# Four row tiles at once while the weights stream in, and a new order of the first Strassen group

## The chip, the cores and the metric

One core of one Trainium2 chip. The metric is the device time of one execution in microseconds; lower is better. "Faster" and "slower" as verdicts need 2%, which is 30 us here; everything below is about differences of 1 to 10 us, and is settled by the profile more than by the clock on the wall.

## The reference

```python
# x: [8, 2048, 2048] float32, w: [2048, 2048] float32
cs = np.cumsum(x, axis=1)
diff = cs - np.concatenate([zeros, cs[:, :-1, :]], axis=1)   # this is x again
return np.matmul(diff, w)
```

So it is one matmul of 16384 x 2048 by 2048 x 2048. Its rows are cut into 128 tiles of 128 rows, numbered 0 to 127.

## The kernel before

The kernel has two parts. While w comes in (16.8 MB), the first row tiles are multiplied plainly, in bf16, piece by piece of w. Then w is scaled to fp16 in four blocks B11, B12, B21, B22, differences T1 to T4 of them are made, and from tile 4 on groups of four row tiles (g, g+1, and h = g+2, h+1) go through a Strassen-Winograd scheme. The first group of four (tiles 4 to 7) is `group_plain`; the other 30 are `group`, which the change does not touch.

`after(engine, ask)` fixes the order in which an engine is given its instructions; the engine then takes them strictly in that order. The parts that matter, before:

```python
EARLY = 3; PLAIN = EARLY + 1
...
for h in range(2):                       # the two halves of w's columns
    ps = [[bank(2 * r + n) for n in range(2)] for r in range(EARLY)]   # six of eight banks
    for ko in range(KO - KQ):
        ...
            if ko == KQ:                 # three quarters of x are turned here, in one go
                for q in range(1, 4):
                    turn_x(q, cast_x(q))
            taken(h, ko)                 # ScalarE casts a piece of w, VectorE takes its maximum
        ...
        for r in range(EARLY):
            plain(h, r, ko)
    ...
# then: tile 3 is turned alone, and multiplied by the scaled blocks (64 matmuls)
V, X = ([bank(i + n) for n in range(2)] for i in (6, 0))
for a in range(2):
    for h in range(2):
        for k in range(KH):
            for n in range(NH // NB):
                nc.tensor.matmul((V, X)[h][n], late_x[:, a * KH + k, :], ...)
...
inpool = ctx.enter_context(tc.tile_pool(name="inner", bufs=1))   # 30 KB a partition
...
cpool = ctx.enter_context(tc.tile_pool(name="C", bufs=1))        # 16 KB: four result tiles
```

## Time and profile before

| | before |
|---|---|
| median of the first runs | 1515.4 us |
| span of the profiled execution | 1513.5 us |
| first useful matmul | 9.6 us |
| first group starts / ends (TensorE) | 82.7 / 132.0 us |
| from there to the end | 1381.5 us |

TensorE is busy 99% of the span, so with its work unchanged there is little to win but what it loses at the start and the end. The stages, TensorE's timeline and the casts that feed it are shown in the prediction below. The page's line of the transposes tells how fast they land over the whole kernel, and the view of tile xT how fast those of tiles 4 to 6 did (60 to 92 us):

```profile
xT<-fin SPq DMA_TRANSPOSE x184, 5.0
DMA to landing us min/median/max: 3.2/4.2/4.9
```

(output and input, issuing queue, kind, count, median us from issue to landing).

### The profile page before, as it was taken

Reading aid. Unit: us, or ns where it says so; the run is one execution under the profiler, and the core shown is the slowest. Engines: PE = TensorE matmul, PEld = TensorE weight load, DVE = VectorE, ACT = ScalarE, POOL = GpSimd, SP = SyncE. Lnnn points to the kernel's source line nnn. Section 1 sums busy time; section 2 is a strip of 40 time slices with the busy share of each in tenths; the row PEclk is TensorE's granted clock in tenths of the full one; section 3 lists DMA queues with packets and bytes.
Section 4 is the critical chain, followed back from the end, with each engine's and each line's share of the span. In section 5 each row is a group of like instructions: output and inputs, shape, how many; then the busy total and the mean of one; then the engine's idle time right before and its main releaser. Section 6 shows DMA issues by size and latency. Waiting matters only on the chain.

```text
span 1513.5 us, 19104 instructions
## 1 busy us (share of the span) xinstructions
PE 1494.7 (99%) x6912; PEld 676.1 (45%) x6912; DVE 1104.6 (73%) x2059; ACT 863.5 (57%) x1099; POOL 10.3 (1%) x21
## 2 busy tenths in 40 slices
PE   7999999999999999999999999999999999999998
PEld 3444444444444444444444444444444444444443
DVE  7987777676777676776767776767776767777767
ACT  6856555556555656555656555665556565556551
POOL 0200000000000000000000000000000000000000
PEclk9999999999999999999999999999999999999999
DMA  9979878878888878888788788788787878887772
GB/s 360 369 191 245 240 219 238 224 221 230 235 239 221 232 221 237 215 251 229 211 233 250 213 246 214 233 235 238 221 236 213 231 226 238 240 234 220 221 207 111
DMA packets 321470, 351.49 MB, mean 232 GB/s; under 512 B 266848, under 2 KB 266848, under 8 KB 305376
## 3 DMA queue, kind: packets, MB, share of 16 engines
q1 hardware_dynamic: 319808, 345.56, 79.7%
q0 software_dynamic: 1280, 4.20, 0.8%
q8 instruction: 54, 0.88, 0.2%
q10 hardware_dynamic: 288, 0.52, 0.1%
q14 instruction: 40, 0.33, 0.1%
HBM read 150.99 MB, written 134.22 MB: 188 GB/s over the span
## 4 chain that ended last, share of the span: by engine, by line
PE 88%; DVE 1%; DMA 1%; issue 0%; ACT 0%; DVEq 0%; ACTq 0%; SPq 0%
PE b L423 52%; PE b L434 35%; DVE c L457 1%; DMA fin<-in_x_dram 0%; DMA xT<-fin 0%; DVE W L466 0%; ACT b L508 0%; DVEq L882 0%; DVE u L541 0%; DVE m L516 0%; DVE m L112 0%; DVE s L113 0%; DVE xT L466 0%; DVEq L457 0%; ACTq L508 0%
## 5 line engine op out<-in xcount | busy, mean ns | idle before, releaser
L457 DVE SCALAR_TENSOR_TENSOR c<-b,u,c 128x512 f32<-128x512 f32 (+1 forms) x883 | 674.9, 799 | 237.9 <-ACT c L452 114.1
L452 ACT ACTIVATE c<-b,u 128x512 f32<-128x512 f32 x496 | 315.0, 680 | 281.2 <-PE b L423 191.1
L423 PE MATMUL b<-W,xT 128*128 128x512 f16 x2048 | 462.4, 379 | 1.0 <-ACT c L452 1.0
L423 PE MATMUL b<-W,W 128*128 128x512 f16 x1764 | 411.9, 379 | 0.0
L106 ACT ACTIVATE c<-fin 128x2048 f16<-128x2048 f32 x92 | 175.7, 1910 | 240.6 <-DMA out_dram<-c 226.0
L423 PEld LDWEIGHTS <-xT 128*128 128x128 f16 x2048 | 200.4, 98 | 243.1 <-issue 1.9
L423 PEld LDWEIGHTS <-W 128*128 128x128 f16 x2016 | 197.3, 98 | 238.1 <-issue 0.3
L117 ACT ACTIVATE fin<-fin,s 128x2048 f16<-128x2048 f32 x123 | 246.2, 2001 | 90.7 <-issue 51.2
L434 PEld LDWEIGHTS <-W 128*128 128x128 f16 x1560 | 152.2, 98 | 187.2 <-issue 2.1
L434 PE MATMUL b<-W,W 128*128 128x512 f16 x810 | 220.0, 379 | 1.0 <-DVE c L457 0.9
L434 PE MATMUL b<-W,xT 128*128 128x512 f16 x720 | 179.9, 379 | 0.0
L434 PE MATMUL b<-inner,W 128*128 128x512 f16 x660 | 176.4, 379 | 0.0
L434 PEld LDWEIGHTS <-xT 128*128 128x128 f16 x960 | 93.9, 98 | 113.3
L516 DVE TENSOR_REDUCE m<-m 128x1 f32<-128x4 f32 x29 | 4.5, 157 | 104.3 <-ACT b L508 104.3
L423 PE MATMUL b<-W 128*128 128x512 f16 x252 | 75.1, 379 | 0.0
L508 ACT ACTIVATE b<-fin 128x512 f32<-128x512 f32 x116 | 67.9, 585 | 11.0 <-DMA fin<-in_x_dram 10.4
L466 DVE TENSOR_TENSOR W<-W,xT 128x1024 f16<-128x1024 f16 x122 | 68.1, 558 | 3.2
L466 DVE TENSOR_TENSOR W<-xT,W 128x1024 f16<-128x1024 f16 x122 | 67.3, 551 | 0.0
L434 PE MATMUL b<-inner,xT 128*128 128x512 f16 x240 | 61.6, 379 | 0.0
L466 DVE TENSOR_TENSOR W<-xT,xT 128x1024 f16<-128x1024 f16 (+1 forms) x92 | 54.8, 595 | 2.2 <-DMA xT<-fin 2.2
L224 PE MATMUL b<-wb,xP 128*128 128x512 bf16 x192 | 45.4, 402 | 3.8 <-ACT wb L212 3.8
L112 DVE TENSOR_SCALAR m<-m 128x1 f32<-128x1 f32 x124 | 18.4, 149 | 39.0 <-ACT c L106 36.3
(59 smaller groups left out, 476.1 us busy)
## 6 DMA issues: line engine op xcount, KB each, us to landing
fin<-in_x_dram SPq DMA_DIRECT2D x124, 1024.0 KB, 5.5
out_dram<-c SPq DMA_DIRECT2D x247, 512.0 KB, 3.1
W<-in_w_dram SPq DMA_DIRECT2D x32, 512.0 KB, 10.3
W<-in_x_dram SPq DMA_DIRECT2D x12, 256.0 KB, 6.3
xT<-fin SPq DMA_TRANSPOSE x184, 5.0
out_dram<-o POOLq DMA_DIRECT2D x10, 256.0 KB, 6.2
out_dram<-wb POOLq DMA_DIRECT2D x6, 256.0 KB, 11.3
xP<-in_x_dram SPq DMA_DIRECT2D x1, 1024.0 KB, 8.5
```

The source lines that it names most:

```text
L106: return m, nc.scalar.activation(waste.bitcast(f16), xf, ABS, scale=1.0 / ROW, accum_out=m)
L112: nc.vector.tensor_scalar(m, m, TINY, None, MAX)
L117: return xh, nc.scalar.activation(xh, xf, COPY, scale=s)
L224: lambda: nc.tensor.matmul(ps[r][n], xP[:, r, ko, :], wb[h, ko][:, ds(n * NB, NB)], start=(ko == 0), stop=(ko == KO - 1),),
L423: nc.tensor.matmul(ps[n], a[k], b[k][:, n, :], start=(first and k == 0), stop=(k == KH - 1), skip_group_check=True,)
L434: nc.tensor.matmul(ps, a[k], b[k], start=(first and k == 0), stop=(k == 3), skip_group_check=True)
L452: after("act", lambda: nc.scalar.activation(c, p, COPY, scale=scale))
L457: "dve", lambda: nc.vector.scalar_tensor_tensor(c, p, scale, c, MUL, ADD)
L466: after("dve", lambda: nc.vector.tensor_tensor(dst.all, p.all, q.all, op))
L508: lambda: nc.scalar.activation(ps[i % 2], xf[:, at], ABS, scale=1.0 / ROW, accum_out=m4[:, i : i + 1],),
L516: after("dve", lambda: nc.vector.tensor_reduce(m, m4, AX.X, ADD))
```

## The change

Its intent: use the eight banks for four row tiles while w streams, seven blocks in the first half of the columns (the eighth bank is for turning x) and eight in the second, so that TensorE has more work per piece than the transfers take; turn the quarters of x between the pieces and not in one go; leave one 128x512 block of tile 3 for later; give the scalings an order in which the first group's first products need only B11 and B21; and reorder the first group. The core of the diff:

```diff
-    EARLY = 3
-    PLAIN = EARLY + 1
+    PLAIN = 4
...
-    name="o", bufs=6
+    name="o", bufs=7
...
+        def here(h, r):
+            return range(1 if h == 0 and r == PLAIN - 1 else 2)
...
+        loads = {0: 0, 2: 1, 5: 2, 9: 3}
+        turns = {2: (1, 0), 3: (1, 1), 5: (2, 0), 6: (2, 1), 9: (3, 0), 10: (3, 1)}
...
+        measure_4(PLAIN, x4)
+        for k in range(4, KH):
+            block(B11, 0, 0, k, "dve")
+        narrow_turn(PLAIN, x4)
+        finish_row(0)
+        for k in range(4):
+            block(B21, 1, 0, k, "dve")
+        measure_4(PLAIN + 2, x6)
+        finish_row(1)
+        ... # load of tile 5 into the room of rows 0 and 1
+        turned_6 = narrow_turn(PLAIN + 2, x6)
+        x7, _ = after("sp", lambda: bring(PLAIN + 3))
+        finish_row(2)
+        ...
+        finish_row(3)
+        with tc.issue_after(turned_6.ins):
+            for c, rows, columns in done:          # eight writes, on GpSimd
+                put(c, rows, columns)
+        for k in range(KH):
+            block(B12, 0, 1, k, "dve")
+        left_over(bank(2))                         # and a ninth
+        ... # measure, narrow and turn tile 5; T1 = B12 - B11
...
+    cpool = ctx.enter_context(tc.tile_pool(name="C", bufs=1))     # C now opens before inner
     inpool = ctx.enter_context(tc.tile_pool(name="inner", bufs=1))
...
         product(X, A11g, B11, True)
+        for k in range(3):
+            block(B22, 1, 1, k, "act")
         C11g = new_c(a)
         keep(C11g, X, ug)
...
         product(V, A12g, B21, True)
-        less(T2, B22, T1)
+        product(Y, A11h, B11, True)                # A11h, A12h: tile 6
+        add(C11g, V, ug)
...
+        product(Z, A12h, B21, True)
...
+        product(V, S1, T1, True)                   # S1: from tile 5
```

## The prediction

> **What bounds the kernel now.** I began with busy time by stages, cutting the span where the timeline of TensorE changes its work: start, stream of w, work between the stream and the first group, first group, the rest.
>
> ```profile
> core 0: us, PE busy (x) PEld busy (x) DVE busy (x) ACT busy (x) POOL busy (x), PEclk, DMA share, GB/s
> 0.00:23.72 23.72, 15.28 (x81) 7.79 (x82) 13.93 (x26) 10.51 (x11) 0.19 (x4) 0.93 0.91 330
> 23.72:61.86 38.14, 38.14 (x168) 16.77 (x167) 36.60 (x38) 32.45 (x36) 5.28 (x9) 0.95 1.02 403
> 61.86:82.68 20.82, 17.68 (x82) 7.86 (x82) 19.11 (x36) 19.23 (x20) 3.06 (x6) 0.84 0.91 259
> 82.68:131.97 49.29, 48.68 (x226) 21.93 (x225) 38.68 (x83) 25.69 (x29) 1.80 (x4) 1.00 0.79 220
> 131.97:149.97 18.00, 17.53 (x81) 7.80 (x80) 13.33 (x39) 14.30 (x22) 0.00 (x0) 1.00 0.90 224
> 149.97:1513.50 1363.53, 1357.38 (x6281) 613.91 (x6279) 982.99 (x1842) 761.32 (x985) 0.00 (x0) 1.00 0.80 226
> ```
>
> The reader should see that from 82.68 us on TensorE is busy all the time at full clock (PEclk 1.00), with VectorE at about 72% and ScalarE at 56% in the last row. That is 94% of the span, and the change touches its code only in the first group. So the change is worth what it saves before about 132 us, and hardly anything else.
>
> Next I read TensorE alone in order of time; the columns are start, length, engine, line, operation, and the idle time before it with its releaser.
>
> ```profile
> 5.98 1.46 PE L184 MATMUL b<-eye,xb 128*128 128x128 bf16 x12 [1.20 <-DVE xb L192]
> 9.63 7.25 PE L224 MATMUL b<-wb,xP 128*128 128x512 bf16 x24 [2.20 <-ACT wb L212]
> 16.72 0.83 PE L184 MATMUL b<-eye,xb 128*128 128x128 bf16 x12
> 18.67 0.84 PE L184 MATMUL b<-eye,xb 128*128 128x128 bf16 x12 [1.12 <-DVE xb L192]
> 20.64 1.46 PE L184 MATMUL b<-eye,xb 128*128 128x128 bf16 x12 [1.12 <-DVE xb L192]
> 23.72 38.14 PE L224 MATMUL b<-wb,xP 128*128 128x512 bf16 x168 [1.62 <-ACT wb L212]
> 62.02 0.62 PE L184 MATMUL b<-eye,xb 128*128 128x128 bf16 x8 [0.16 <-DVE xb L312]
> 63.96 0.62 PE L184 MATMUL b<-eye,xb 128*128 128x128 bf16 x8 [1.31 <-DVE xb L312]
> 66.24 16.60 PE L368 MATMUL b<-W,late 128*128 128x512 f16 x64 [1.66 <-ACT late L316]
> 82.68 13.98 PE L423 MATMUL b<-W,xT 128*128 128x512 f16 x64
> ```
>
> In the group at 82.68, 64 matmuls take 96.49 − 82.68 = 13.81 us (the next record starts at 96.49), so a 512-column matmul costs 0.216 us. Before 82.68 us TensorE does 192 + 64 = 256 of them, which is 55.3 us; 27.4 us are lost. Where: 9.6 before the first useful matmul; 6.8 from 16.88 to 23.72, in which three quarters of x are turned one after another between empty waits; 4.4 from 61.86 to 66.24, turning the fourth row tile; and the rest, 6.4, is cold clock. The weight loads in the same timeline come singly, 0.43 us apart, from 9.63 to 13.43, from 23.72 to 27.09 and from 66.24 to 71.67: about 9, 8 and 13 matmuls with 0.21 us too much each, 1.9 + 1.7 + 2.7. Sum 27.2 of 27.4.
>
> Last I read what feeds TensorE: the casts of w on ScalarE.
>
> ```profile
> 22.62 7.67 ACT L212 CAST wb<-W 128x1024 bf16<-128x1024 f32 x8
> 34.43 1.05 ACT L212 CAST wb<-W 128x1024 bf16<-128x1024 f32 x1 [0.23 <-DMA W<-in_w_dram]
> 55.11 1.05 ACT L212 CAST wb<-W 128x1024 bf16<-128x1024 f32 x1 [0.22 <-DMA W<-in_w_dram]
> ```
>
> Back to back a cast takes 7.67 / 8 = 0.96 us. When it waits it follows the transfers at one piece per 1.28 us; the last piece of the first half of w lands near 34.3 us, the last of all near 55.0. With three row tiles a piece feeds 6 matmuls, 1.30 us: TensorE and transfers are level, so once behind, TensorE has nothing with which to fill a hole.
>
> **What the Trainium skill says.** "TensorE: Matmul & The Clock Gate", Part 1, "Wait — 56ns, not 53.3ns?" has 512-column matmuls start 426.7 ns apart cold and 215.7 ns warm, and the same part lets the clock drop after an idle window of about 3.4 us. The trace agrees: 0.43 and 0.216 us, cold after the two holes above. "Perfetto Trace Analysis", "Identifying the Most-Contended Engine", warns that matmul busy time is no measure of closeness to the roofline: true here, since the row 61.86:82.68 has 17.68 us busy, yet its 64 matmuls are worth 13.8. "VectorE: DVE Perf Modes", "The perf-mode tier table", gives a reduce only the 1x rate and an fp32 scaling 2x: in the trace 1.213 us (1.13 back to back, 16.98 us for 15) against 0.742 for the same 1024 columns. "DMA: Bandwidth & Descriptors", "Measured", has 425 GB/s for 16 MB to one core; the trace shows 403 while w streams, so more bytes there cost time in proportion.
>
> **The change part by part.** TensorE's work is the same: 192 + 64 plain matmuls become 112 (first half of w, 4 row tiles less one block, 7 per piece) + 128 (8 per piece) + 16 (the block left over) = 256; 64 transposes stay 64, only now 16 ahead of the stream and 48 inside it, 8 at a time. So I re-do the sum of losses.
>
> Start: the first quarter of x is now four rows, 1.05 MB instead of 0.79. At some 0.3 MB/us (early slices carry about 300 GB/s) this is +0.8: first useful matmul at 10.4 instead of 9.6. Cold start as before, 1.9.
>
> Transposes in the stream: 12 took 0.83 us, so 8 take about 0.57, six sets 3.4 us, warm.
>
> Waits in the stream: x comes 0.26 MB a quarter heavier, 1.05 MB in all, so at 0.41 MB/us everything lands 2.5 us later: last piece of the first half about 36.9, of all 57.5. With 7 matmuls a piece TensorE needs 1.51 us per 1.28 us of transfer. I walked down the order. For piece 2 the second quarter of x lands near 13.8, its two casts take 1.0 to 1.4, then ScalarE casts w: 0.7 us wait. At pieces 4 and 7 ScalarE has to copy a turned half (1.0) ahead of the cast (1.0), more than TensorE's 1.5: 0.5 us each. At pieces 12 to 15 the row-wise order asks for piece 15 within 1.3 us, but it is cast by 37.9, when TensorE has come to about 36.6: 1.3 us. Between the halves ScalarE alone empties the seven banks (two 0.53 us copies a row, after three casts): 1.0 us. Sum 4.0. The second half of w is then bound by TensorE, 1.73 us per piece, so transfers, casts (0.96) and reduces (1.13) are hidden.
>
> So the first group starts at 10.4 + 1.9 + 3.4 + 4.0 + 55.3 = 75.0 us, instead of 82.7. The hole at 62 to 66 us with its cold clock (7.1) and that at 17 to 24 (8.5 with the cold clock) go; 0.8 + 3.4 + 4.0 come in. 15.6 − 8.2 = 7.4, which agrees within rounding.
>
> First group: the same 224 matmuls, 48.4 us. Before it lost only 131.97 − 82.68 − 48.4 = 0.9. Now the scaling of w starts later (1.0 after the last reduce near 58.7, so 59.9) but is needed sooner. VectorE from 59.9: 24 scalings by 0.70 = 16.8, small operations and their waits 1.5, T1 8 × 0.61 = 4.9, two scalings 1.4, two adds 1.4, two differences 1.2, the sum S1 0.7: 87.8 us, and that without waiting for x. TensorE has four products that need none of it (13.8 us) and asks for S1 at 75.0 + 13.8 = 88.8. The row tile for S1 is loaded late (its room is freed by the second row), measured only after the left-over block (near 75.7 to 77.7), narrowed and turned: 80 + 2.0 + about 5.5 = 88. Level, so I put 1 us there, and 1 us for S4g, which stands behind all of T2 on VectorE: 2.0 in place of 0.9. The group ends at 75.0 + 48.4 + 2.0 = 125.4, against 131.97.
>
> Sum: −6.6 us. 1515.4 − 6.6 = 1508.8.
>
> **The rivals.** *All waits vanish.* If ScalarE and the transfers never stop TensorE, losses are 10.4 + 1.9 + 3.4 and the group starts at 71.0 and keeps its 0.9: about 12.8 less, 1502.6. For it: the kernel is tuned, and my 4.0 is from a walk by hand. Against: ScalarE has 23 operations in the first half, by 0.96 about 22 us of 27, in a fixed order.
> *VectorE becomes the bound of the first group.* It was 78% busy there (38.68 of 49.29) and has no slack by my sum; if a wait for x holds its queue for 3 to 4 us, T2 and S4g slip with it: 1511 to 1513. For it: strict order, and scalings of B12 that left ScalarE. Against: the six blocks of B22 go to ScalarE, which was 52% busy.
> *Transfers bound the stream.* 1.05 MB more before the last piece; if TensorE followed the transfers all through, its gain would shrink to nothing. Against: the last cast near 58.4 comes long before TensorE reaches that piece (its last 32 matmuls start near 64). That time at the end is hidden; only the 1.3 us at piece 15 are seen. Full loss: 1515.
>
> **Range and chances.** The floor is 1502.6, no gain 1515.4; the middle rival is likelier than the extremes. 1504.5 to 1512.5 for 8 in 10. Two per cent is 30 us, more than all 27.4 us lost before the first group, so faster by over 2% is next to impossible, and slower by over 2% would need a stall that repeats in every group, of which nothing in the change speaks: 0.01 each.
>
> **What would show it.** TensorE's useful matmuls starting near 10.4 us, no cold stretch after the first, transposes in sets of 8 without holes over 1 us, the 16 left-over matmuls ending near 75, the first group ending near 125 with holes below 1 us ahead of S1 and S4g, and an unchanged span from there (1381.5 us). I am wrong if a hole over 3.4 us brings the cold clock back, if the left-over block waits for B21, or if the second group loses over 1 us more than now.

## More of the kernel before

`ring` (casts of w), `o` (finished rows) and `first` (x turned, and so on) are pools that are closed before `inner` and `C` open; these take over their memory.

Every run here can be compared, by its ratio to the kernel before of its own rounds; the 95% interval of a ratio is 0.0015 to 0.0021 to either side, 2.3 to 3.2 us.

## The result

1514.3 us (median of four runs, 1513.17 to 1515.17) against 1515.35: the ratio is 0.9992, with a 95% interval of 0.9975 to 1.0009. (A ratio is the mean time of one kernel's fast runs over that of the other's of the same rounds, so not quite the ratio of the medians.) "Same" was right, but the time lies outside the range of 1504.5 to 1512.5: 1 us was won where 6.6 were predicted, and as the interval includes 1, even that is not clear of the noise.

The profiled execution was the quickest of the four (1513.17, span 1511.4 us). Its stages, cut at the first useful matmul, the end of the left-over block and the end of the first group:

```profile
core 0: us, PE busy (x) PEld busy (x) DVE busy (x) ACT busy (x) POOL busy (x), PEclk, DMA share, GB/s
0.00:11.48 11.48, 6.58 (x24) 2.53 (x25) 4.38 (x12) 3.34 (x3) 0.19 (x4) 1.00 0.80 263
11.48:76.20 64.72, 61.70 (x299) 28.19 (x305) 56.81 (x66) 53.33 (x70) 9.13 (x14) 1.00 0.98 371
76.20:129.90 53.70, 50.35 (x226) 22.24 (x225) 43.43 (x89) 34.81 (x37) 2.57 (x4) 0.97 0.85 228
129.90:1511.40 1381.50, 1374.93 (x6361) 621.72 (x6359) 999.77 (x1888) 775.31 (x1007) 0.00 (x0) 1.00 0.80 226
```

The last row lasts 1381.5 us, exactly as before: the whole story lies ahead of 129.9 us, as predicted. The work up to the first group is done by 76.2 us (predicted 75.0, before 82.7). But the first group then takes 53.7 us for 48.4 us of matmuls (predicted 50.4, before 49.3). Of 6.5 us won, over four are given back. TensorE's timeline of the changed kernel says where:

```profile
11.48 5.09 PE L233 MATMUL b<-wb,xP 128*128 128x512 bf16 x14 [0.77 <-ACT wb L216]
...
39.08 33.51 PE L233 MATMUL b<-wb,xP 128*128 128x512 bf16 x147 [0.35 <-ACT wb L216]
72.72 1.04 PE L463 MATMUL b<-W,xT 128*128 128x512 f16 x4
73.59 3.62 PE L373 MATMUL b<-W,xP 128*128 128x512 f16 x16
77.04 6.21 PE L463 MATMUL b<-W,xT 128*128 128x512 f16 x28
86.60 8.77 PE L463 MATMUL b<-W,xT 128*128 128x512 f16 x32 [3.35 <-DMA xT<-fin]
95.20 0.59 PE L463 MATMUL b<-W 128*128 128x512 f16 x2
```

No hole from 39 to 83 us: the stream of w is as it was meant to be. Then 3.35 us of standing still ahead of the third product, for a turned tile ("DMA xT<-fin": tile 6). After it, 32 matmuls take 95.20 − 86.60 = 8.60 us instead of 6.91: 1.7 us of cold clock. (The four matmuls at 72.72 are the first of the group, let in ahead of the 16 of the left-over block; so I count the group from 77.04 − 4 × 0.216 = 76.2.)

The view of tile xT from 60 to 80 us gives the transposes of tiles 4 and 6, and its last line their landing:

```profile
L127 SPq DMA_TRANSPOSE xT<-fin x2: 2015/3426/4836, 67.2 to 74.1; - x2
DMA to landing us min/median/max: 5.5/9.0/12.5
```

Tile 4 lands 5.5 us after its issue, like any; tile 6, issued at 74.1, takes 12.5 us. And ScalarE's timeline shows a second wait:

```profile
82.21 3.21 ACT L334 ACTIVATE W<-W,uinv 128x1024 f16<-128x1024 f32 x3
89.35 1.26 ACT L492 ACTIVATE c<-b,u 128x512 f32<-128x512 f32 x2 [3.93 <-DMA out_dram<-o]
```

This is the first C tile, C11g. The room of the pool C is that of `ring` and the first `o` buffer, and the wait in the program is for all nine writes. They are issued by GpSimd:

```profile
71.95 1.25 POOL L243 DMA_DIRECT2D out_dram<-o  x2 [2.11 <-ACT o L251]
74.81 3.02 POOL L243 DMA_DIRECT2D out_dram<-o  x4 [1.62 <-ACT o L251]
78.22 0.93 POOL L243 DMA_DIRECT2D out_dram<-o  x1 [0.39 <-ACT o L382]
```

The last one, issued at 78.2, landed 11.0 us later, at 89.25, and ScalarE goes on at 89.35. VectorE, strictly in order, stood 3.49 us behind C11g.

### The profile page after: what moved, and what is told of

Its sections match the earlier page's. It is cut to its first block, busy times and chain, and to the rows that moved or that the text cites. A ratio compares the mean times of both kernels' runs of the same rounds, so it can differ in the third digit from the quotient of the medians.

```text
span 1511.4 us, 19128 instructions
## 1 busy us (share of the span) xinstructions
PE 1493.6 (99%) x6906; PEld 674.7 (45%) x6912; DVE 1104.4 (73%) x2052; ACT 866.8 (57%) x1116; POOL 11.9 (1%) x21
## 4 chain that ended last, share of the span: by engine, by line
PE 89%; DVE 1%; issue 0%; DVEq 0%; ACT 0%
PE b L463 53%; PE b L474 36%; DVE c L497 1%; DVE W L506 0%; DVE W L510 0%; DVEq L929 0%; ACT b L548 0%; DVE xT L506 0%; DVE s L112 0%; DVE m L111 0%; DVE u L581 0%; DVE m L556 0%; DVEq L497 0%
## 5 line engine op out<-in xcount | busy, mean ns | idle before, releaser
L506 DVE TENSOR_TENSOR W<-W,xT 128x1024 f16<-128x1024 f16 x122 | 68.1, 558 | 3.2
L233 PE MATMUL b<-wb,xP 128*128 128x512 bf16 x234 | 56.0, 388 | 3.7 <-ACT wb L216 2.9
```

The source lines that it names most:

```text
L233: lambda: nc.tensor.matmul(ps[r][n], xP[:, r, ko, :], wb[h, ko][:, ds(n * NB, NB)], start=(ko == 0), stop=(ko == KO - 1),),
L506: after("dve", lambda: nc.vector.tensor_tensor(dst.all, p.all, q.all, op))
```

## The experiments

**Theory A**: the writes of finished rows share the transfer engines with the transposes of tile 6 and hold them up. **Theory B**: the transposes are late because they are issued late and stand behind the load of tile 5 in the same queue. **Theory C**: VectorE has too much to do before S1. Since chips differ a little, the gain over the kernel before of the same rounds is what is compared (the changed kernel: 0.9992, twice).

### Without the writes

```diff
-        with tc.issue_after(turned_6.ins):
-            for c, rows, columns in done:
-                put(c, rows, columns)
...
-            put(c, ds((PLAIN - 1) * P, P), ds(NB, NB))
```

> The changed kernel without the nine writes of finished rows that go out between 68 and 79 us (eight of the second half of w, one of the block left over); rows 0 to 3 of the result are wrong on purpose. In the changed kernel the transposes of row tile 6 are issued at 74.1 us and land at 86.5, and TensorE stands 3.35 us for them and then runs some 8 matmuls at the cold clock. Theory A (those writes share the transfer engines with the transposes and delay them): they land near 80, the hole before the third product and the cold stretch go, the first group ends near 125 instead of 129.9, and the time falls by 4 to 5 us. Theory B (the transposes are late because they are issued late and stand behind the load of row tile 5 in the same queue): they still land after 84, a hole of 1 us or more stays, and the time falls by under 2 us.

Its output is wrong, which doesn't matter for the time. 1508.93 us against 1516.18 of before in the same rounds, ratio 0.9952. The first two transposes:

```profile
DMA to landing us min/median/max: 4.4/5.1/5.9
```

Tile 6, issued at 73.8 us, lands 5.9 us later instead of 12.5, and no wait for it is left. It was still issued late and still behind the load of tile 5, so B falls: it is the writes that delay tile 6, as A says (how they do it is looked at below). But this edit also frees C11g, so it cannot say how much each of the two waits costs.

### A ring of eight, so that C lies on the ring alone

```diff
-        name="ring", bufs=7
+        name="ring", bufs=8
...
-        waste = first.tile([P, NB], f16, name="waste")
+        waste = T1[0][:, 0, :]
```

> One more buffer in the ring (and the throw-away output of the measuring put elsewhere to make room), so that the first result tile C11g no longer lies on the room of the finished rows and need not wait for their writes (in the changed kernel 3.9 us, until 89.35). If the hole before the third product is what binds (A and B alike), VectorE gets on about 3.5 us sooner but TensorE doesn't: within 1 us of the changed kernel. If instead the queue of VectorE behind C11g binds the first group (theory C), 2 to 4 us faster than the changed kernel.

1511.41 us, ratio 0.9968: about 3.5 us better than the changed kernel, in all of its four executions (1511.13 to 1511.58), against my expectation under A. The trace shows that the edit did more than intended:

```profile
71.75 1.24 POOL L243 DMA_DIRECT2D out_dram<-o  x2 [1.18 <-ACT o L251]
74.61 7.12 POOL L243 DMA_DIRECT2D out_dram<-o  x5 [1.62 <-ACT o L251]
```

One write stayed 5.0 us on GpSimd (74.6 to 79.6), so the four after it left only when it was done. With the writes held off, though not by design, tile 6 landed in 7.9 us, before TensorE asked for it. That fits A, but makes this run useless for weighing the wait of C11g. C11g did not wait here, and yet TensorE stood 1.67 us ahead of the fifth product: VectorE waited 1.92 us for the transposes of tile 5, which landed 7.7 and 7.1 us after their issue, against 3.2 in the run without the writes. So the writes hold up tile 5 too. (In the changed kernel its second half landed only at 91.1 us, so even without the wait of C11g the sum S1 could not have started before that; it started at 92.6.) Why that one write took 5.0 us is open.

### Tile 6 first

```diff
+        narrow_turn(PLAIN, x4)
         for k in range(4, KH):
             block(B11, 0, 0, k, "dve")
-        narrow_turn(PLAIN, x4)
+        measure_4(PLAIN + 2, x6)
+        turned_6 = narrow_turn(PLAIN + 2, x6)
         finish_row(0)
...
         finish_row(1)
         ... # load of tile 5
-        turned_6 = narrow_turn(PLAIN + 2, x6)
```

> Row tile 6 is measured and narrowed straight after row tile 4, before the finished rows are copied out, and its transposes go ahead of the load of row tile 5 and of the writes. A and B: issued near 72, landed near 78 to 80, no hole before the third product. But then the wait of C11g for the writes (until about 89) shows: S1 near 93, a hole of about 3 us before the fifth product and perhaps the cold clock there. Faster than the changed kernel by 1 to 2 us only. If nothing stands behind C11g, by 5.

1516.97 us, ratio 1.0005: no gain, a miss. No transpose took over 5.7 us to land, and the hole ahead of the third product was gone. But the edit put the load of tile 5 behind those transposes, so it was issued at 74.4 us instead of 69.3 and shared the engines with the writes:

```profile
84.44 1.91 ACT L414 ACTIVATE xP<-xP 128x2048 f16<-128x2048 f32 x1 [6.04 <-DMA xP<-in_x_dram]
```

ScalarE measured tile 5 at 84.4 instead of 77.8 us. VectorE's next instruction wanted that measure (5.46 us idle), all of T1 and S1 stood behind it, and TensorE's hole merely moved to the fifth product:

```profile
77.52 12.90 PE L463 MATMUL b<-W,xT 128*128 128x512 f16 x59
96.38 1.03 PE L463 MATMUL b<-W 128*128 128x512 f16 x2 [5.96 <-DVE W L506]
```

### Both of these

The diffs of the last two together.

> Both of the two edits before together. A or B with the wait of C11g as second lock: no hole over 1 us up to the fifth product, no cold stretch there, the first group ends near 125, 4 to 5 us faster than the changed kernel (about 1509). Theory C (VectorE simply has too much work before S1): a hole of 2 us or more stays before the fifth product and the gain is under 3 us.

1516.9 us, ratio 1.0003. The same hole of 6.2 us ahead of the fifth product. As C11g did not wait here, the hole belongs to tile 5 alone. The bound that I had called "VectorE has too much work" (C) looks like this, but it is a queue standing for one late load: the work itself fits, as the run with held writes shows.

### The changed kernel again

No edit.

> The changed kernel again, unedited, to have its time and trace on the same chip as the next two. Theory A: hole before the third product of 1 to 4 us and 8 or so cold matmuls after it, C11g waiting until 87 to 90 us; time 1 to 2.5 us under the kernel before, as first measured (its four runs were 1513.2, 1513.5, 1515.1, 1515.2).

1514.46 us (1512.28 to 1515.35), ratio 0.9992 again.

```profile
76.49 6.21 PE L463 MATMUL b<-W,xT 128*128 128x512 f16 x28
87.17 9.64 PE L463 MATMUL b<-W,xT 128*128 128x512 f16 x32 [4.47 <-DMA xT<-fin]
96.64 0.59 PE L463 MATMUL b<-W 128*128 128x512 f16 x2
```

The hole is 4.47 us here, the 32 matmuls after it 9.47 us (2.6 of it cold), and tile 6 landed after 13.4 us. From 75.6 to the group's end at 131.2 it lost 7.2 us. This execution's span was 1.5 us longer than that of the one first profiled: the group lost 1.9 more and began 0.6 earlier.

### Held writes and the ring of eight

The seven writes from the `o` buffers go into the sync engine's own queue, behind the transposes of tile 5, where they cannot leave early. C must then not lie on an `o` buffer, hence the ring of eight.

```diff
         (ring of eight as above)
...
         with tc.issue_after(turned_6.ins):
-            for c, rows, columns in done:
+            for c, rows, columns in done[:2]:
                 put(c, rows, columns)
+        held = done[2:]
...
-            put(c, ds((PLAIN - 1) * P, P), ds(NB, NB))
+            held.append((c, ds((PLAIN - 1) * P, P), ds(NB, NB)))
...
         narrow_turn(PLAIN + 1, x5)
+        for c, rows, columns in held:
+            after("sp", lambda: nc.sync.dma_start(out2[rows, columns], c))
```

> The ring of 8, and seven of the nine writes of finished rows (those from the o buffers) not issued by GpSimd as they get ready but put into the sync engine's queue behind the transposes of row tile 5, so that they can't share the transfer engines with those of row tile 6. Correct result. Theory A: transposes of tile 6 land within 6 us of their issue (near 80), no hole before the third product, as in the run without those writes, and the time comes within 1 us of that run, 6 to 7.5 us under the kernel before. If the writes only move the trouble (the load of row tile 8 and the first C tile then queue behind 1.8 MB), a hole of over 1 us turns up later in the first group and the gain is 4 us or less.

Correct, 1509.47 us (1508.97 to 1509.97), ratio 0.9963; 5.0 us under the changed kernel on the same chip. This is the quickest correct version, with the warm start below. The ring of eight alone had 0.9968, so beside it the held writes add less than the noise.

```profile
72.74 3.62 PE L373 MATMUL b<-W,xP 128*128 128x512 f16 x16
76.19 13.11 PE L466 MATMUL b<-W,xT 128*128 128x512 f16 x60
89.14 0.59 PE L466 MATMUL b<-W 128*128 128x512 f16 x2
```

```profile
DMA to landing us min/median/max: 5.6/6.0/6.5
```

Tile 6 lands in 6.5 us; the first four products run through, and the fifth follows at once: VectorE has S1 in time (its sum ends at 88.9 us, TensorE asks at 89.1). So C falls: the work fits as soon as nothing stands in the queue. The first group ends at 122.06 + 16 × 0.216 = 125.5 us.

Counting bytes in the traces by queue in slices of 2 us from 72 us on, each packet where it starts, shows the two meeting. "writes" are GpSimd's, "turned" the packets under 512 bytes of the sync engine's queue, which are the transposes; "loads" the large packets of that queue (GB/s; the held writes themselves, in packets of 2 KB from 84 us on, are left out):

```
from                         72   74   76   78   80   82   84   86
changed kernel    writes     63  102  258   61   84  184  276   49
                  loads     160  266   41    0    0    4  139  348
                  turned      0    0   54  142   39   27    0   12
again             writes     80  137  215   61   33  215  297   43
                  loads     213  242    4    0    0    0   86  373
                  turned      0    0   70  128   35   29    1    6
without writes    loads     401    4   33  336  156    0   29  266
                  turned      0  108  154    0    0  106  157    0
held writes       writes    121   35    0    0    0    0    0    0
                  loads     283  168   49  287  188    0    0    0
                  turned      0   76  187    0    0  130  133    0
```

Tile 6 (0.52 MB) is through in two slices where no writes are under way, and is spread over four, 76 to 84, where they are. Without writes the load of tile 5, which stands ahead of it in the queue, was over by 74 us; in the changed kernel it shared with the writes and lasted until 76 or longer. So the writes cost tile 6 twice: what stands ahead of it gets slower, and then so does it.

This is not a mere sharing of bandwidth. From 80 to 82 us writes and transposes of the changed kernel together moved 123 GB/s, with packets under way all the time (DMA share 1.45), less than the transposes' part alone in the best slice with held writes (187). The 256-byte packets of the transposes take 18 ns in the median, with the writes and without; but beside the writes single ones of tile 6 took up to 1.1 us, and in the run without writes none over 0.1 us. What holds them is open. Nor does a run tell whether it is the bytes of the writes or their coming from a second queue, that of GpSimd: after the first group all results are written through the sync engine's own queue, and in the kernel before no transpose took over 8.2 us.

### Work in the hole

```diff
         product(V, A12g, B21, True)
+        for k in range(8):
+            for n in range(2):
+                nc.tensor.matmul(Z[0], A12g[k], B21[k][:, n, :], start=True, stop=True, ...)
         product(Y, A11h, B11, True)
```

> The changed kernel with 16 useless matmuls (into a bank that the fourth product clears) between the second and the third product, 3.45 us of work where TensorE stood for 3.35 us. If the hole costs its own length plus a cold stretch (8 matmuls by 0.21 us, 1.8 us), then filling it with work keeps the clock up and the kernel gets FASTER by 1 to 2 us although it does more. If there is no cold penalty, it stays equal; if tile 6 lands earlier than in the first trace in most executions, it gets slower by up to 3.4 us.

1513.99 us (1511.69 to 1516.0), ratio 0.9992. In the profiled execution the useless work filled the hole, 0.38 us were left of it, the next 32 matmuls took 6.92 us (warm), and the time was 1511.69 us, the lowest of its four. But the other three runs took 1513.8 to 1516.0, and the median is 0.5 us under the changed kernel's: that the cold clock costs about 2 us of the whole time is shown by single traces, not by this median. Inconclusive as a timing.

### Control: only the throw-away output moved

```diff
-        waste = first.tile([P, NB], f16, name="waste")
+        waste = T1[0][:, 0, :]
```

> Control for the run with the ring of 8, which had two edits: here only the throw-away output of the measuring is moved, the ring stays at 7. In the run with the ring of 8 one write on GpSimd took 5.0 us and the four after it went out only from 79.6 us, and tile 6 landed 7.9 us after its issue instead of 12.5 to 13.4. If that came from moving the throw-away output, it shows again here: tile 6 under 9 us, time 3 to 4 us under the kernel before. If it came from the ring (other memory for C and the o buffers), this run is like the changed kernel: landing 12 to 13.5 us, hole of 3 to 4.5 us, time within 1 us of it.

1513.97 us (one of four runs took 1520.6), ratio 0.9997: like the changed kernel. Tile 6 landed after 12.8 us, with a hole of 3.64 us. So the gain of the ring of eight came with the ring's size. In this execution the 32 matmuls after the hole were warm (86.62 to 93.54 us): whether a hole of this length brings the cold clock varies (3.35 us: 1.7 us of it; 4.47: 2.6; 3.64: none).

### Control: held writes without the ring of eight

> The held writes without the ring of 8. Tile 6 lands within 6 us and the third and fourth products follow at once, but C11g must wait for the held writes, which leave from about 84 us and land near 89 to 91: then VectorE's queue stands, S1 comes near 94 to 95 and TensorE has a hole of 4 to 6 us before the fifth product, with a cold stretch after it. If this second lock is real: 3 us or more slower than the run with both edits, about the time of the changed kernel. If C11g's wait is harmless: as fast as with both edits.

1518.62 us, ratio 1.0018.

```profile
77.36 13.11 PE L466 MATMUL b<-W,xT 128*128 128x512 f16 x60
97.70 1.03 PE L466 MATMUL b<-W 128*128 128x512 f16 x2 [7.23 <-DVE W L509]
```

```profile
93.72 1.27 ACT L495 ACTIVATE c<-b,u 128x512 f32<-128x512 f32 x2 [7.98 <-DMA out_dram<-o]
```

No hole ahead of the third product (no transpose took over 6.0 us), but C11g waited until 93.7 us for the held writes, VectorE with it, and TensorE stood 7.2 us ahead of the fifth product. The second lock is real: held writes pay only if C does not lie on what they write from. The two runs with held writes lie 0.9963 and 1.0018 of before, about 8 us apart, for one more buffer in the ring and the harmless move of the control.

### A warm start

The held writes with the ring of eight, and:

```diff
+            for i in range(6 - 4 * a):     # after each turned half of the first quarter
+                ... nc.tensor.matmul(bank(0), xb[:, 0, :P], xb[:, 0, :NB], start=True, stop=True)
```

> The run with both edits (held writes, ring of 8) and eight useless matmuls more at the start, six after the first turned half of x and two after the second, where TensorE otherwise idles at 7 to 9.7 us and before the first piece of w. If the cold start of the stream (about 9 matmuls by 0.21 us) comes from those idle stretches, it becomes warm and the kernel is 1 to 2 us faster than with both edits; if the first useful matmul is held up by them, equal or slower.

1509.78 us, ratio 0.9959: equal to the run without it (0.9963).

```profile
11.37 3.18 PE L233 MATMUL b<-wb,xP 128*128 128x512 bf16 x14
14.39 0.61 PE L195 MATMUL b<-eye,W 128*128 128x128 bf16 x8
16.52 1.67 PE L233 MATMUL b<-wb,xP 128*128 128x512 bf16 x7 [1.52 <-ACT wb L216]
```

The first 14 matmuls are warm now, 3.18 us instead of 4.57 in the run without it (5.09 in the changed kernel). TensorE then waits 1.52 us for the third piece of w to be cast, for whose transfer ScalarE had waited 2.91 us: warm or cold, the transfers decide when the third piece starts. The cold start costs nothing here. (This stream began 2 us later than that of the run without it, as the second half of x landed at 8.75 and not at 6.85 us; that varies from execution to execution, so the comparison rests on the medians.)

## Why the prediction was wrong

**What bounds the kernel, and where a gain can come from**: right. The 1381.5 us after the first group did not change by a tenth in the first trace (1381.7 in the second; 1382.4 with held writes, where 0.9 us of the gain went again).

**The stream of w**: right in kind, 1.2 us too good. The left-over block ended at 76.2 us (75.6 in the second trace), predicted 75.0. In the first trace two terms were off and nearly cancel: the start (first useful matmul at 11.48, not 10.4) and the waits for casts (2.9 us, not 4.0); some 0.9 us of small gaps stand in no term. The second half of the first quarter of x landed only by 8.9 us. This varies: in the run with held writes the stream began at 9.38 us, yet the block ended at 75.3, because waits for casts in the stream made up for it (4.7 us there). So the sum behaves better than its terms, which is luck and not knowledge. And the run with the warm start shows that the cold start (1.9) and the wait for the third piece are not two terms to be added.

**The first group**: here it failed. The prediction says: "TensorE has four products that need none of it (13.8 us) and asks for S1 at 75.0 + 13.8 = 88.8." Two of those four products need tile 6, and its arrival is not in the sum at all. I had checked the chain of tile 5 to 0.5 us and not that of tile 6. It has the same links (row finished, measured, narrowed, turned) and one that no trace of the kernel before showed: transposes with 1.8 MB of writes beside them. In the kernel before, the transposes of tiles 4 to 6 landed in at most 4.9 us; there the writes of finished rows were issued by 65.7 us and had landed by 75.3, the first transpose was issued at 72.7, and the four writes of tile 3, issued from 82.3 us on, moved nothing before 84, when tile 6, issued at 80.4 and landed at 84.7, was nearly through. The term "2.0 in place of 0.9" measured 5.3 in the first trace and 7.2 in the second: a hole of 3.35 or 4.47 us, and 1.7 or 2.6 us of cold clock. That is where the predicted gain went: turned into a new wait, by contention.

The run with held writes checks the rest of the sum: without the contention, and without C11g's wait, the group ended at 125.5 us where the prediction has 125.4, and its loss was 125.5 − 75.3 − 48.4 = 1.8 where the prediction has 2.0. That the two losses agree is luck: ahead of S1 and S4g, where the prediction put 1 us each, TensorE lost 0.1 us or less, and 1.4 us stand ahead of the thirteenth product, whose bank ScalarE had not emptied, as it had waited 1.84 us for the load of tile 9. (The expectation for this run named such a hole. It is 1.07 us without the writes too, so holding them did not make it; in neither trace of the changed kernel does TensorE stand there.) Its time is 0.9963 of before, 5.6 us less; predicted 6.6.

**"VectorE becomes the bound of the first group"**: the rival named the right symptom, "if a wait for x holds its queue for 3 to 4 us". It did hold, 3.5 us, but for C11g, that is for the writes and not for x. In the changed kernel this was hidden: TensorE stood for tile 6 meanwhile. It shows alone where the first lock is opened (the control with held writes only).

**"Transfers bound the stream"**: the last pieces were hidden, as argued. But transfers bounded the next stage, of which the prediction did not think: it treated them as a matter of the stream alone.

**Chances**: 0.98 for "same" was sound. The range was too narrow on its upper side, as its top assumed that at most one chain would slip by 3 to 4 us. Its floor rests on a wrong sum: with the group starting at 71.0 and losing 0.9 it would end at 71.0 + 48.4 + 0.9 = 120.3, which is 11.7 less than 131.97 and not 12.8, so 1503.7 and not 1502.6.

**The clock**: the two rates, 0.43 and 0.216 us, are right. That the clock drops after an idle window of about 3.4 us is not what the trace cited there shows: in the hole at 62 to 66 us the longest single idle stretch is 1.66 us, with transposes in between, and yet the clock was at half from 66 to 70 us. And of the three holes ahead of the third product the one of 3.64 us brought no cold clock.

**Left open**: how much of the cold clock shows in the median (the run with work in the hole spread over 4 us), and why one write took 5.0 us with the ring of eight.

## What to carry to other kernels

When a change reorders the work between two stages, list for every product each operand's whole chain to its landing, also the ones that used to be early; a transpose's landing time measured in a quiet stage did not hold beside a burst of writes (4.9 us at most against 12.5). Writes that nobody waits for should be put in the queue behind the loads and transposes that somebody does wait for, and their source buffers must not be what the next stage's first tile is laid on. After opening one lock look for the next in the same stretch: here tile 6 first, or the held writes alone, gained nothing or lost; the ring of eight alone gained about 3.5 us, and with the held writes 5.

## What the Trainium skill lacked or had wrong

- "DMA: Bandwidth & Descriptors", "Latency and other measured facts" gives 261 GB/s for a DMA transpose, 350 to 400 when contiguous. Here 0.52 MB landed 5.9 us after issue with no writes beside it (89 GB/s with all latency; the best 2 us slice of the kernel before, 76 to 78 us, moved 237 GB/s, near the page's figure), and 12.5 to 13.4 us beside seven writes of 0.26 MB. What the page says of a transpose in company is about corruption and hangs; it has no figure for its time beside ordinary writes.
- "SBUF — State Buffer", "Who interferes with whom" says that VectorE in a two-port mode and GpSimd's descriptor writing lock each other out. In one kernel a write on GpSimd took 5.0 us while VectorE ran twelve fp32 scalings from 71.5 to 79.5 us, which would fit; in the changed kernel, beside the same twelve scalings (71.7 to 79.7 us), seven writes took 0.6 to 1.0 us each. The page says that whoever issues first holds the ports for its whole instruction; a scaling took 0.67 us, so this alone does not give 5.0.
